# Moving the start of the weights' and the activations' buffers on the chip to multiples of 512 bytes, in a hybrid decoder layer

## The chip, the cores and the metric

The kernel runs on one core of a Trainium2 chip. The metric is the device time of one launch in microseconds, the median of several runs. Names of engines: PE is the matrix engine (PEld its weight load), DVE the vector engine, ACT the scalar engine, POOL the general engine, SP the engine that here only issues DMAs.

## The reference

One decoder layer on 256 tokens of width 2048, all in float32: a norm, one wide input projection, three branches (latent attention, gated linear attention, gated delta net), a gated merge of their projections, an output projection with residual, and a gated channel mixer with a causal convolution. Cut to the products, which are nearly all of the work:

```python
def token_mixer(h, ...):
    parts = jnp.split(h @ w_in, _split_points(), axis=-1)        # 2048 x 13408
    ...
    mixed = (g_mla * (y_mla @ w_branch_mla) + g_gla * (y_gla @ w_branch_gla)
             + g_gdn * (y_gdn @ w_branch_gdn))                   # three times 1024 x 2048
    return mixed @ w_out                                         # 2048 x 2048

def conv_ffn(h, w_up, conv_w, conv_b, w_down):
    gate, up = jnp.split(h @ w_up, 2, axis=-1)                   # 2048 x 11264
    gate = causal_dwconv(gate, conv_w) + conv_b
    return (jax.nn.silu(gate) * up) @ w_down                     # 5632 x 2048
```

## The kernel before, in words

Every large product is made of three: weights and activations are each split into a high and a low part of the type float32r (`hi`, `lo`), and high by high, high by low and low by high are added up in PSUM. A piece of weights is two k-tiles of 128 rows by 512 columns (`KP = 2`): SP loads it as `raw` (L183, helper `piece`), ACT casts `hi` (L190) and DVE takes `lo = raw - hi` (L103 through `tt`), and PE multiplies. `raw`, `hi` and `lo` have four buffers each in the pool `stream`. Three helpers issue the products:

- `t_chunk` (L246 to L248), tokens on the output's partitions: the stationary operand is a 128 x 128 block of the activations, the moving one 128 x 512 of the weights in `stream`. A chunk of 16 k-tiles is 96 matmuls. The whole program has 1,280 matmuls on each of the three lines.
- `fj_chunk` (L227, L228), for the up projection of the channel mixer: the stationary operand is a block of the weights in `stream`, the moving one the activations `hl_h`, 512 columns (high and low side by side) on L227 and 256 on L228, in turn. 1,408 pairs.
- `f_chunk` and others through `mm3` (L195 to L197), and the key and value products of the latent attention (L491 to L493): stationary blocks from `stream`, 256 moving columns from the activations, or the reverse; 492 matmuls on each of L195 to L197, 32 on each of L491 to L493.

A fourth loop stands at the end (L1165 to L1167): the last quarter-chunk of the down projection, 4 k-tiles, whose split weights `wl` were put into the buffers of the activations' pools beforehand, so that both of its operands come from there; 512 columns at a time for three quarters of the width, then twice 256, for each of the two token tiles.

On the chip a tile is a range of bytes in every one of 128 partitions. Pools lie one behind the other in the order in which they are opened: `const` (tiles made by `keep`), `stream`, `small` (tiles made by `small`), and then `slots`, `slots2` and the region pools, which hold all activations in slots of 2 KiB and, for some, 1 or 1.5 KiB. In the built program `stream` begins at byte 24,992 of the partition, which is 48 x 512 + 416, and `slots` at byte 85,024, which is 166 x 512 + 32. A slot of 2 KiB and a block of 128 columns of float32 (512 bytes) keep the offset within 512 bytes, so nearly every operand from `stream` begins at 416 and nearly every operand from the activations' pools at 32 modulo 512. In the last loop (L1165 to L1167) both operands begin at 32.

The order of instructions on each engine is set by the Tile framework's scheduler, which runs a simulated timeline when the program is built; it is not written by hand.

Of the kernel before, what the change touches and what calls it, by code (L numbers as in the profile page):

```python
# [16 lines left out]
P = 128  # L17
# [4 lines left out]
NSMALL = 5  # GLA levels within 32 positions  # L22
WARM = 8
FFN_PARTS = ((0, 4), (4, 8), (8, 10))  # of the 11 chunks of 512; the last one is left over
KP = 2  # k-tiles in a piece of weights

# column offsets of the combined input projection
# [5 lines left out]
def shape_constants():  # L33
    """Masks and tables that depend on the shapes alone: float columns and 0/1 masks."""
    i = np.arange(P)[:, None]
    j = np.arange(P)[None, :]
    ident = (i == j).astype(np.float32)
    tri = (i <= j).astype(np.float32)
    gt = (i > j).astype(np.float32)
    amask = np.where(j <= i, 0.0, -1e30).astype(np.float32)  # L40
    inv = 10000.0 ** (-np.arange(0, 64, 2, dtype=np.float64) / 64)
    cols = np.zeros((P, 2))
    cols[:, 0] = np.tile(inv, 4)
    cols[:, 1] = np.where((np.arange(P) % 64) < 32, -1.0, 1.0)
    # within a diagonal 32 x 32 block [j, i], twice: the identity and the levels' halves
    bj, bi = i % 32, np.tile(np.arange(32), 2)[None, :]
    masks = [bj == bi]
    for l in range(NSMALL):
        s = 1 << l
        masks.append((bi // (2 * s) == bj // (2 * s)) & ((bi // s) % 2 == 1) & ((bj // s) % 2 == 0))  # L50
    reset = np.broadcast_to(np.arange(T) % 64 != 0, (P, T))
    return (np.concatenate([ident, tri, gt, amask, cols], axis=1).astype(np.float32),
            np.concatenate(masks + [reset], axis=1).astype(np.float32))


def trunk(ctx, tc, A, out, dbg=None, stop=None):
# [14 lines left out]
    # Slots of 2 KiB a partition. A tag's slots are given out in program order, so that work which  # L71
    # runs side by side has tags of its own; the pools of the region follow each other on its bytes.
# [37 lines left out]
    def rsqrt(m, n):  # L110
        """[P, n] positive -> 1/sqrt, by the bit-level start and Newton steps."""
        y = small(n, "rsy", 4)
        dve.tensor_scalar(y.bitcast(I32), m.bitcast(I32), -0.5, 1597463007.0, op0=MUL, op1=ADD)
        mh = small(n, "rsm")
        dve.tensor_scalar(mh, m, -0.5, None, op0=MUL)
        for _ in range(3):
            a = small(n, "rsa")
            tt(a, y, y, MUL)
            tt(a, a, mh, MUL)
            y2 = small(n, "rsy", 4)  # L120
            stt(y2, a, 1.5, y, ADD, MUL)
            y = y2
        return y
# [4 lines left out]
    # ---------------------------------------------------------------- constants  # L128
# [3 lines left out]
    ident = keep([P, P], "ident")  # L132
# [22 lines left out]
    # the tensor engine's clock rises while the first loads are on their way  # L155
# [20 lines left out]
    # ---------------------------------------------------------------- weights  # L176
# [22 lines left out]
    def f_chunk(wv, c0, actv, n=512):  # L199
        """feature-major: list of PSUM banks, two [128, 256] tiles in each"""  # L200
        nf = n // P
        banks = [ACC() for _ in range((nf + 1) // 2)]
        nk = len(actv)
        for k0 in range(0, nk, KP):
            kk = min(KP, nk - k0)
            hi, lo = piece(wv[:, k0:k0 + kk, c0:c0 + n], kk, n)
            for f in range(nf):
                o = banks[f // 2][:, (f % 2) * 256:(f % 2) * 256 + 256]
                for kt in range(kk):
                    k = k0 + kt  # L210
                    ah, al = actv[k]
                    fs = slice(f * P, (f + 1) * P)
                    mm3(o, hi[:, kt, fs], lo[:, kt, fs], ah, al, k == 0 and f % 2 == 0, k == nk - 1)
        return banks

    def fj_chunk(wv, c0, joint, tag):
        """feature-major, by the joint parts [high | low] of 256 tokens each: a PSUM bank for each of four
        tiles, whose halves add up to the product"""
# [13 lines left out]
    def t_chunk(wv, c0, actv, n=512, ks=None):  # L232
        """token-major: one PSUM bank [128 tokens, n] for each token tile"""
# [20 lines left out]
    def pairs(n, tag, name):  # L254
        """n feature tiles [128, 256], two in each slot"""
        tiles = [S(tag, (P, 2, 256), n=name) for _ in range((n + 1) // 2)]
        return tiles, [tiles[i // 2][:, i % 2, :] for i in range(n)]

    class Act:
        """activations [n k-tiles of 128, 256 tokens] as the exact sum of two fp32r parts"""  # L260
# [11 lines left out]
        def add(self, full):  # L272
            """full: [128, 2, 256] fp32, the next two k-tiles"""
            hi, lo = self.new()
            act.copy(hi, full)
            tt(lo, full, hi, SUB)
# [4 lines left out]
    class Joint(Act):  # L281
        """the same with both parts of a k-tile in one slot"""
# [9 lines left out]
    def gained(psb, gains, store):  # L292
        """PSUM bank with two k-tiles [128, 256], times a per-partition gain each, split"""
# [8 lines left out]
    # ---------------------------------------------------------------- norm of x  # L302
    def row_stats(tiles, n):
        """tiles[t][c] [128, 512] -> sum of squares [128, 2]"""
# [14 lines left out]
    def row_bcast(r, o):  # L319
        """[128, 2] of the two token tiles -> [128, 256], the same on every partition"""  # L320
# [12 lines left out]
    # x times the gain of its norm; the rows' 1/rms comes in after the projections  # L333
# [36 lines left out]
    # ---------------------------------------------------------------- MLA projections  # L370
    # rotary tables on 4 groups of 32 partitions
# [52 lines left out]
    # rotary key, GLA's low-rank gate, GDN's beta and decay logits: one tile of 96 columns  # L424
# [11 lines left out]
    def rope(o, x, nq):  # L436
        """o[:32 nq] = rotary of x; x at the same partitions, in PSUM or at 0..63"""
# [16 lines left out]
    for hp in range(4):  # L454
        b0, b1 = ACC(), ACC()
        for k0 in range(0, 4, KP):
# [4 lines left out]
            # columns put in the order nope, nope, rope, rope  # L461
# [37 lines left out]
    # ---------------------------------------------------------------- MLA attention  # L499
# [49 lines left out]
    # ---------------------------------------------------------------- GDN projections  # L549
# [25 lines left out]
    # ---------------------------------------------------------------- GDN mixing  # L575
# [9 lines left out]
    def b3(ap, n):  # L585
        """[P, a] -> [P, a, n], repeated"""
# [18 lines left out]
    # sums of squares of q and k: row i for the i-th pair of tiles, then token-major  # L605
# [37 lines left out]
    # decay between positions j <= i from segment sums of the log decay: within the first and the second  # L643
    # half, and (second half's prefix) + (first half's suffix, as the exponential's bias)
# [40 lines left out]
    for g in range(4):  # L685
# [10 lines left out]
        # decayed q k of the blocks 00, 01 | 11 and decayed k k of the block 01, for both heads  # L696
# [10 lines left out]
    # inverses of the 32 x 32 unit-triangular diagonal blocks, transposed, by forward substitution:  # L707
    # partitions = (half of the columns, block, unit)
# [32 lines left out]
    # two groups of heads side by side, so that one's steps fill the other's waits  # L741
    for gp in ((0, 1), (2, 3)):
        # values token-major, over the norm of k
# [66 lines left out]
    # per-head norm: f = s rsqrt(s^2 ssq / 128 + eps)  # L810
# [13 lines left out]
    def gated_out(o_tiles, f_of, zs, gcol, name, ytag):  # L824
        """o token-major times its norm factor and gate -> feature-major, times gain, split"""
# [15 lines left out]
    def gates_of(c0, name, tag):  # L841
        """token-major 2 silu(z) / r of 1024 columns z of the input projection, r the rows' 1/rms"""
# [10 lines left out]
    # ---------------------------------------------------------------- merge  # L853
# [3 lines left out]
    def merge(b, y, w, c, first=False, last=False):  # L857
        """512 columns of a branch's projection, times its gate, into the sum"""
# [39 lines left out]
    # ---------------------------------------------------------------- GLA projections  # L898
# [15 lines left out]
    # ---------------------------------------------------------------- GLA mixing  # L914
# [6 lines left out]
    # log gates feature-major, and their running sums from each start of 64 positions  # L921
# [23 lines left out]
    def halves(ap, s):  # L945
        """[P, 256] -> the left and the right halves [P, blocks, s] of blocks of 2 s"""
# [5 lines left out]
    for hd in range(4):  # L952
        q, k, cb = lqv[hd], lkv[hd], sums[hd]
        # exponents: from each block's middle, and of the two chunks from the boundary between them
# [24 lines left out]
        # products [j, i]: diagonal 32 x 32 blocks of the small levels and of q k itself, then levels 5 and 6  # L979
# [64 lines left out]
    # ---------------------------------------------------------------- output projection, residual  # L1044
# [39 lines left out]
    # ---------------------------------------------------------------- channel mixer  # L1084
# [56 lines left out]
    # the last part goes by token tiles, so that the first one's norm and stores run under the second's  # L1141
    # products; its weights stay on chip
# [14 lines left out]
    for t in range(2):  # L1157
# [22 lines left out]
        # three Newton steps for -8 / sqrt(m): y <- (y y m / 4^i - 3) y is -2 times the usual one  # L1180
# [60 lines left out]
```

## Time and profile before

| | |
|---|---|
| time, median of 3 runs | 1707.05 us (1706.93 to 1707.15) |
| span of the profiled execution | 1705.8 us, granted PE clock 0.997 of full speed |
| around the span | 1.25 us between it and the median of the runs |
| busy share of the span: PE, PEld | 99%, 84% |
| DVE, ACT, POOL | 64%, 48%, 5% |
| DMA | 308.71 MB, 181 GB/s mean |

A profiled execution has no device time of its own beside its span, so the sums below are made against the span of 1705.8 us and then put on the median of the runs. "Busy" for PE counts from a matmul's start to its modelled end, and the ends overlap the next starts: the duration of one matmul is no measure of what it costs. What it costs is the distance from its start to the next start, and that is read from the timeline.

### The profile page before, as it was taken

What the parts mean: (1) busy time and instruction counts of PE and PEld (TensorE: products, weight loads), DVE (VectorE), ACT (ScalarE), POOL (GpSimd) and SP (SyncE); (2) the same over time, 40 slices, a digit from 0 to 9 for tenths busy, and PEclk for the clock granted to TensorE, in tenths of its full rate; (3) what the DMA queues carried; (4) which work ended last, traced back from release to release, by engine and by line L of the source; (5) the groups of instructions that cost most, each with busy time, mean ns of one, the idle gap of its engine ahead of it and who ended that gap; (6) DMA issues with size and microseconds to landing.
All of it is one profiled execution on the core that took longest, in us unless ns stands there. A gap on an engine that the chain in (4) does not pass through costs nothing.

```text
span 1705.8 us, 24609 instructions
## 1 busy us (share of the span) xinstructions
PE 1692.2 (99%) x9516; PEld 1438.3 (84%) x9516; DVE 1095.1 (64%) x1709; ACT 819.0 (48%) x1132; POOL 88.9 (5%) x132
## 2 busy tenths in 40 slices
PE   9999999999999999999999999999999999999997
PEld 7999988878988788888888888888888888888886
DVE  6856887855744695655555666664466665466666
ACT  6554553333444564444444455553355553345454
POOL 1000013200000000000000000000000000000000
PEclk9999999999999999999999999999999999999999
DMA  7554456654455465556655666655565556655653
GB/s 259 156 187 136 149 161 185 200 156 146 153 185 185 150 196 172 173 179 205 197 196 186 201 187 189 191 186 186 187 193 188 185 186 188 193 186 186 189 186 119
DMA packets 166277, 308.71 MB, mean 181 GB/s; under 512 B 16826, under 2 KB 19570, under 8 KB 166160
## 3 DMA queue, kind: packets, MB, share of 16 engines
q1 hardware_dynamic: 163200, 301.83, 56.4%
q0 software_dynamic: 2928, 5.30, 1.1%
q8 instruction: 74, 1.21, 0.3%
q14 instruction: 43, 0.35, 0.1%
q10 hardware_dynamic: 32, 0.01, 0.0%
HBM read 304.48 MB, written 2.62 MB: 180 GB/s over the span
## 4 chain that ended last, share of the span: by engine, by line
PE 99%; DMA 0%; ACT 0%; DVE 0%; SPq 0%; ACTq 0%; issue 0%
PE acc L247 18%; PE acc L248 18%; PE acc L246 18%; PE acc L227 10%; PE mix L227 10%; PE acc L228 5%; PE mix L228 5%; PE acc L197 3%; PE acc L195 3%; PE acc L196 3%; PE ps L511 0%; PE acc L1165 0%; PE acc L1167 0%; PE acc L1166 0%; PE ps L510 0%; DMA x<-in_x_dram 0%
## 5 line engine op out<-in xcount | busy, mean ns | idle before, releaser
L103 DVE TENSOR_TENSOR lo<-raw,hi 128x1024 fp32r<-128x1024 f32 (+2 forms) x571 | 687.1, 1205 | 540.7 <-ACT hi L190 537.5
L190 ACT CAST hi<-raw 128x1024 fp32r<-128x1024 f32 (+2 forms) x555 | 581.1, 1047 | 753.8 <-PE acc L248 437.1
L247 PE MATMUL acc<-lo,hi_h 128*128 128x512 f32 x640 | 254.0, 398 | 0.0
L248 PE MATMUL acc<-hi,lo_h 128*128 128x512 f32 x640 | 252.7, 397 | 0.0
L246 PE MATMUL acc<-hi,hi_h 128*128 128x512 f32 x640 | 251.4, 397 | 0.7 <-ACT hi L190 0.7
L227 PE MATMUL mix<-hl_h,hi 128*128 128x512 f32 x704 | 247.7, 393 | 0.0
L227 PE MATMUL acc<-hl_h,hi 128*128 128x512 f32 x704 | 247.5, 394 | 0.0
L228 PE MATMUL mix<-hl_h,lo 128*128 128x256 f32 x704 | 199.1, 283 | 0.0
L228 PE MATMUL acc<-hl_h,lo 128*128 128x256 f32 x704 | 198.6, 283 | 0.0
L227 PEld LDWEIGHTS mix<-hl_h,hi 128*128 128x128 f32 x704 | 132.2, 188 | 30.5
L227 PEld LDWEIGHTS acc<-hl_h,hi 128*128 128x128 f32 x704 | 131.9, 188 | 30.1
L246 PEld LDWEIGHTS acc<-hi,hi_h 128*128 128x128 f32 x640 | 120.7, 189 | 29.0 <-ACT hi L190 1.3
L247 PEld LDWEIGHTS acc<-lo,hi_h 128*128 128x128 f32 x640 | 120.9, 189 | 27.7 <-DVE lo L103 0.4
L248 PEld LDWEIGHTS acc<-hi,lo_h 128*128 128x128 f32 x640 | 120.6, 189 | 27.3
L228 PEld LDWEIGHTS acc<-hl_h,lo 128*128 128x128 f32 x704 | 132.3, 188 | 0.6
L228 PEld LDWEIGHTS mix<-hl_h,lo 128*128 128x128 f32 x704 | 132.4, 188 | 0.0
L247 PE MATMUL acc<-lo,hi_f 128*128 128x512 f32 x320 | 126.1, 394 | 0.0
L246 PE MATMUL acc<-hi,hi_f 128*128 128x512 f32 x320 | 125.9, 395 | 0.0
L248 PE MATMUL acc<-hi,lo_f 128*128 128x512 f32 x320 | 125.7, 394 | 0.0
L197 PE MATMUL acc<-hi_h,lo 128*128 128x256 f32 (+1 forms) x400 | 113.6, 284 | 0.0
L195 PE MATMUL acc<-hi_h,hi 128*128 128x256 f32 (+1 forms) x400 | 113.6, 284 | 0.0
L196 PE MATMUL acc<-lo_h,hi 128*128 128x256 f32 (+1 forms) x400 | 113.4, 284 | 0.0
(390 smaller groups left out, 2238.8 us busy)
## 6 DMA issues: line engine op xcount, KB each, us to landing
raw<-in_w_in_dram SPq DMA_DIRECT2D x207, 512.0 KB, 3.5
raw<-in_ffn_w_up_dram SPq DMA_DIRECT2D x176, 512.0 KB, 4.1
raw<-in_ffn_w_down_dram SPq DMA_DIRECT2D x88, 512.0 KB, 4.6
raw<-in_w_out_dram SPq DMA_DIRECT2D x32, 512.0 KB, 3.8
raw<-in_w_branch_mla_dram SPq DMA_DIRECT2D x16, 512.0 KB, 3.7
raw<-in_w_branch_gdn_dram SPq DMA_DIRECT2D x16, 512.0 KB, 3.7
raw<-in_w_branch_gla_dram SPq DMA_DIRECT2D x16, 512.0 KB, 3.8
raw<-in_mla_w_ukv_dram SPq DMA_DIRECT2D x8, 512.0 KB, 4.4
```

Of the source, the lines that this page charges most:

```text
L103: (eng or dve).tensor_tensor(o, a, b, op=op)
L190: act.copy(hi[:, ks], raw[:, ks])
L195: pe.matmul(o, s_hi, m_hi, start=first, stop=False, skip_group_check=True)
L196: pe.matmul(o, s_hi, m_lo, start=False, stop=False, skip_group_check=True)
L197: pe.matmul(o, s_lo, m_hi, start=False, stop=last, skip_group_check=True)
L227: pe.matmul(banks[f], hi[:, kt, fs], joint[k], start=k == 0, stop=False, skip_group_check=True)
L228: pe.matmul(banks[f][:, :T], lo[:, kt, fs], joint[k][:, :T], start=False, stop=k == nk - 1, skip_group_check=True)
L246: pe.matmul(o, ah, hi[:, kt, :], start=first, stop=False)
L247: pe.matmul(o, ah, lo[:, kt, :], start=False, stop=False)
L248: pe.matmul(o, al, hi[:, kt, :], start=False, stop=last)
```

## The change

One tile of the pool `const` is made 24 columns (96 bytes) wider, of which the first 128 columns are used as before, and one tile of 95 columns is added to the pool `small` and set to zero by POOL, so that it is used at all. Apart from these two lines the change takes away comments and docstrings.

```diff
-    ident = keep([P, P], "ident")
+    ident = keep([P, P + 24], "ident")[:, :P]
+    pool.memset(small(95, "room", 1), 0.0)
     sync.dma_start(ident, cst[:, 0:P])
```

In the built program `stream` now begins at byte 25,088 = 49 x 512 and `slots` at byte 85,504 = 167 x 512, and all slots of the activations at the same distances behind it as before; what begins at 416 and what begins at 32 modulo 512 now begins at 0. Tiles of `const` move by 96 bytes (except `ident` itself). One line is added, so lines from 133 on have numbers greater by one.

The scheduler gives the same instructions on SP in the same order. On PE, DVE and ACT the order differs only in the first part of the program, up to the rotary tables and the query latent; from there on all rows are the same. Three places of that follow.

ACT, the first casts and normalised activations, before (`hi_318` is the high part of the first weights, `hi_h_140` and `hi_h_151` the first activations, `junk` the sum of squares of x):

```order
L650 CAST maskr<-ones 128x128
L649 CAST maskr<-rest 128x128
L309 ACTIVATE junk_224,st_223<-x_106 128x512
L299 ACTIVATE hi_h_140<-ps_135,ac 128x256
L190 CAST hi_318<-raw_110 128x512
L299 ACTIVATE hi_h_151<-ps_146,ac 128x256
L190 CAST hi_318<-raw_110 128x512
L299 ACTIVATE hi_h_140<-ps_135,ac 128x256
```

and now:

```order
L651 CAST maskr<-ones 128x128
L310 ACTIVATE junk_226,st_225<-x_108 128x512
L191 CAST hi_320<-raw_112 128x512
L300 ACTIVATE hi_h_142<-ps_137,ac 128x256
L191 CAST hi_320<-raw_112 128x512
L300 ACTIVATE hi_h_153<-ps_148,ac 128x256
L300 ACTIVATE hi_h_142<-ps_137,ac 128x256
```

The first weight cast now stands ahead of the first activation instead of behind it, and the copy of `rest` has left this place (it comes later on ACT).

POOL, the first DMAs, before (`rest` holds masks and the rotary columns, `prow` the gains):

```order
L1237 UNCONDITIONAL_BRANCH
L145 DMA rest<-in_cst_dram 128x386
L141 DMA prow_82<-in_ffn_norm_dram 16x128
L141 DMA prow_82<-in_mla_q_norm_dram 4x128
L141 DMA prow_82<-in_mla_kv_norm_dram 4x128
```

and now:

```order
L1238 UNCONDITIONAL_BRANCH
L133 MEMSET room_79 128x95
L142 DMA prow_84<-in_ffn_norm_dram 16x128
L142 DMA prow_84<-in_mla_q_norm_dram 4x128
L142 DMA prow_84<-in_mla_kv_norm_dram 4x128
L142 DMA prow_84<-in_gla_out_norm_dram 8x128
L142 DMA prow_84<-in_gdn_out_norm_dram 8x128
L142 DMA prow_84<-in_gdn_conv_w_dram 64x128
L146 DMA rest<-in_cst_dram 128x386
```

The memset is new at the head of the queue, and the load of `rest` has gone behind the six loads of `prow`.

## Rows read from the trace of the kernel before

**Rows 1.** The page's parts 1 and 4: busy time, chain that ended last

```profile
PE 1692.2 (99%) x9516; PEld 1438.3 (84%) x9516; DVE 1095.1 (64%) x1709; ACT 819.0 (48%) x1132; POOL 88.9 (5%) x132
...
PE 99%; DMA 0%; ACT 0%; DVE 0%; SPq 0%; ACTq 0%; issue 0%
```

**Rows 2.** Waits of PE: us in total, times, longest

```profile
PE acc L1165 <- ACT hi_f L275: 1.1, 1, 1.1
PE warm L158 <- DVE ones L154: 1.1, 1, 1.1
PE ps L340 <- DMA x<-in_x_dram: 0.7, 1, 0.7
PE acc L246 <- ACT hi L190: 0.7, 1, 0.7
```

**Rows 3.** Timeline of PE: start us, us; `t_chunk`'s stretch of 384 matmuls, first and last

```profile
483.42 0.39 PE L246 MATMUL acc<-hi,hi_h 128*128 128x512 f32 x1
...
572.41 0.39 PE L248 MATMUL acc<-hi,lo_h 128*128 128x512 f32 x1
```

**Rows 4.** The same for `fj_chunk`: first of 512 pairs, next line's first start

```profile
1223.79 0.40 PE L227 MATMUL acc<-hl_h,hi 128*128 128x512 f32 x1
...
1403.52 0.40 PE L246 MATMUL acc<-hi,hi_f 128*128 128x512 f32 x1
```

**Rows 5.** Windows: us; PE, PEld, DVE, ACT, POOL busy (x); PEclk, DMA share, GB/s

```profile
460.00:483.00 23.00, 23.00 (x196) 23.00 (x195) 12.65 (x16) 9.99 (x13) 0.00 (x0) 1.00 0.58 186
484.00:572.00 88.00, 88.00 (x381) 71.32 (x380) 43.26 (x39) 37.41 (x39) 0.00 (x0) 1.00 0.61 189
1230.00:1400.00 170.00, 170.00 (x970) 149.00 (x969) 112.61 (x142) 89.28 (x120) 11.33 (x8) 1.00 0.60 188
1688.00:1692.00 4.00, 4.00 (x19) 3.30 (x18) 3.49 (x16) 2.01 (x8) 0.00 (x0) 1.00 0.00 0
```

**Rows 6.** Timeline of PE in the last loop, second token tile

```profile
1687.44 0.40 PE L1165 MATMUL acc<-wl,hi_f 128*128 128x512 f32 x1
1687.68 0.40 PE L1166 MATMUL acc<-wl,hi_f 128*128 128x512 f32 x1
1687.91 0.39 PE L1167 MATMUL acc<-wl,lo_f 128*128 128x512 f32 x1
...
1688.61 0.39 PE L1167 MATMUL acc<-wl,lo_f 128*128 128x512 f32 x1
1688.83 0.39 PE L1165 MATMUL acc<-wl,hi_f 128*128 128x512 f32 x1
...
1692.91 0.28 PE L1165 MATMUL acc<-wl,hi_f 128*128 128x256 f32 x1
...
1693.14 0.28 PE L1167 MATMUL acc<-wl,lo_f 128*128 128x256 f32 x1
...
1695.66 0.28 PE L1167 MATMUL acc<-wl,lo_f 128*128 128x256 f32 x1
```

**Rows 7.** Timeline of PE: shortest distances in `fj_chunk` and in the last loop

```profile
1002.20 0.39 PE L227 MATMUL acc<-hl_h,hi 128*128 128x512 f32 x1
1002.42 0.28 PE L228 MATMUL acc<-hl_h,lo 128*128 128x256 f32 x1
...
1685.53 0.28 PE L1166 MATMUL acc<-wl,hi_f 128*128 128x256 f32 x1
1685.64 0.28 PE L1167 MATMUL acc<-wl,lo_f 128*128 128x256 f32 x1
```

**Rows 8.** Timelines of ACT and POOL: the start, and a memset of POOL

```profile
6.94 0.47 ACT L299 ACTIVATE hi_h<-ps,ac 128x256 fp32r<-128x256 f32 x1 [0.42 <-PE ps L340]
7.31 0.61 ACT L190 CAST hi<-raw 128x512 fp32r<-128x512 f32 x1
...
7.30 0.17 POOL L607 MEMSET sel<- 128x68 f32 x1
```

## The prediction

> **What bounds the kernel.** I read the page first: PE is busy for 99% of the span and the chain that ended last is PE for 99% [rows 1]. Then the waits of PE: four of them, 3.6 us in all, at the very start and at the last loop [rows 2]. So no transfer, cast or subtraction decides the time; only what one matmul costs does. [...]
>
> - `t_chunk`, 512 columns: 384 matmuls, 383 distances in 572.41 - 483.42 = 88.99 us [rows 3], 0.2324 us each (0.23235 unrounded).
> - `fj_chunk`, 512 and 256 columns in turn: 512 pairs in 1403.52 - 1223.79 = 179.73 us [rows 4], 0.3510 us a pair.
> - 256 columns from L195 to L197: 196 matmuls touch the window from 460 to 483 us [rows 5], two of which began before it; 194 in 23.00 us is 0.1186 us.
> - The last loop, once it has settled: 18 matmuls of 512 columns in 1692.91 - 1688.83 = 4.08 us, 0.2267 us each, and 21 of 256 columns in 1695.66 - 1693.14 = 2.52 us, 0.1200 us each [rows 6].
>
> The last loop is what I build on. It does the same three products as `t_chunk`, with operands of the same shapes and types, and takes 5.7 ns less for each. DVE is busy for 3.49 of 4.00 us beside it, more densely than beside `t_chunk` [rows 5], so idle neighbours are not the reason. Two things differ: its weights lie in the activations' pools, so that the moving and the stationary operand both begin at 32 modulo 512, where `t_chunk` streams from 416 against blocks at 32; and no DMA runs beside it (share 0.00 against 0.61) [rows 5]. The difference between the two widths, 226.7 - 120.0 = 106.7 ns for 256 columns, is 0.417 ns a column, one per period of 2.4 GHz; so every matmul pays something on top of its columns: 13.3 ns in the last loop, 232.35 - 213.3 = 19 ns in `t_chunk`, (351.0 - 320.0) / 2 = 15.5 ns in `fj_chunk`, 118.6 - 106.7 = 12 ns on L195 to L197. The change can move only this part, and it is paid some 8,200 times.
>
> **The change part by part.** My theory is that the part on top depends on where the two operands begin relative to each other within 512 bytes, because the next weight load reads while the columns stream. After the change all of them begin at 0, so their relation is that of the last loop, and I give them its numbers.
>
> - `t_chunk`: 3 x 1,280 = 3,840 matmuls, 232.35 to 226.67 ns, gives 3,840 x 5.68 = 21.8 us less. Settling costs something: after a change of width the last loop took 1688.83 - 1687.44 = 1.39 us for six [rows 6] against 1.36. At most 40 chunks have to settle, 40 x 0.03 = 1.2 us; I take 1.5.
> - `fj_chunk`: 1,408 pairs, 351.04 to 226.67 + 120.00 = 346.67 ns, gives 6.2 us less. The widths alternate here, so it may never settle; the bounds are 0 and 6.2 and I take 6.2, since in the last loop the long first distance after a change of width (0.24) and the short one the other way (0.11) [rows 6, 7] nearly cancel.
> - L195 to L197 and L491 to L493: 3 x 492 + 3 x 32 = 1,572 matmuls, 118.6 to 120.0 ns, 2.2 us more; bounds 0 and 2.2.
> - The weights' DMAs now land at multiples of 512 bytes. Whatever that gives them is hidden: PE waited for a DMA once, 0.7 us, for x at the start [rows 2]. I cost it at nothing; it could give back those 0.7 us at most.
> - The memset on POOL: the nearest row is one of 128 x 68 at 0.17 us [rows 8]; the six loads of `prow` start that much later, and `rest` behind them about 3 us later. Their users come tens of microseconds later on PE. Nothing, unless ACT should stand at the copy of `rest`.
> - The order at the start: ACT's first cast of weights now stands ahead of the first activation. ACT idled for 0.42 us before that activation and the cast takes 0.61 us [rows 8]. If the weights have landed by then, the first product comes up to 0.6 us earlier; if not, ACT holds the activation back, by perhaps 1 us. I take 0, with bounds of -0.6 and +1.0.
>
> Sum: -21.8 + 1.5 - 6.2 + 2.2 = -24.3 us, so a span of 1681.5 us, and on the median of the runs 1707.05 - 24.3 = 1682.7 us. The bounds of the terms make it 1678 (the 256 columns unchanged, nothing paid for settling, 0.6 and 0.7 us gained at the start) to 1691 (`fj_chunk` unchanged, settling twice as dear, 1 us lost at the start).
>
> **The rivals.**
>
> *No change (about 1707).* The last loop's gain comes from the absent DMA, or from the place of its buffers in the large, or the distances are an affair of PE alone. For it: DMA share and operand offsets change together between the stretches [rows 5], so the trace cannot part them, and engine and DMA are otherwise independent here (PE does not wait). Against it: when the DMA is equally absent, right after a change of width, the distances are 0.24, 0.23 us and settle only later [rows 6], so a quiet DMA does not bring 0.2267 by itself. [...]
>
> *Much faster (about 1616).* Not the relation alone counts but a start at a round address: both before and after, relation or not, every operand of the old kernel begins at 32 modulo 128, so the trace has no row of an aligned one. The best it could show is the shortest distances seen: 0.22 us for 512 columns and 0.11 us for 256 [rows 7]. Then `t_chunk` gives 3,840 x 12.35 = 47.4 us, the pairs 1,408 x 21 = 29.6, the rest 1,572 x 8.6 = 13.5; 90.5 in all. For it: these distances occur, so what is paid on top is not fixed. Against it: the last loop, once settled, does not use them. [...]
>
> *Slower (about 1725).* With both operands beginning at 0, the weight load and the columns meet head-on at every start, and the kernel stays where the last loop is just after a change of width: 1687.91 - 1687.44 = 0.47 us for two, 0.235 each [rows 6]. Then 3,840 x 2.65 = 10.2, pairs of 0.235 + 0.120 us 1,408 x 4 = 5.6, and 2.2 on the rest: 18 us more. The point from which it decides is a mean of 232.35 ns for 512 columns. Against it: the last loop has both operands at the same offset, and settles.
>
> **How the numbers follow.** What a measurement of this kernel can tell from no change is about 0.2%, 3.4 us. Forecast 0.52; no change 0.22; much faster 0.10; slower 0.12; the remaining 0.04 for only one of the terms coming true, between 1691 and 1703. Faster by over 0.2%: 0.52 + 0.10 + 0.04 = 0.66; within: 0.22; slower: 0.12. The range from 1670 to 1710 takes in the forecast with its bounds, the part between, and no change; the forecast's own range is 1678 to 1691.
>
> **What would show it.** In the timeline of the changed kernel, the stretch of 384 matmuls of `t_chunk` should take 87.0 us where it took 89.0, the 512 pairs of `fj_chunk` 177.5 where they took 179.7, and the last loop should be as it was, 0.2267 and 0.1200 us. If the distances are unchanged and the time too, the relation of the offsets was not the cause; if the last loop itself becomes shorter, the absolute start counts; if 512 columns take more than 232.35 ns, the starts collide. PE's waits should stay under 5 us in all; if they grow, I have misjudged the start.

## The result and the profile after

The changed kernel takes 1685.96 us (median of 4 runs, 1684.95 to 1686.28), the kernel before beside it 1707.10 us (1706.93 to 1707.19): a ratio of 0.9873, 95% interval [0.9861, 0.9884], so 21.1 us less. The profiled execution has a span of 1682.8 us where it was 1705.8, 23.0 us less. The forecast was 1682.7 us with a range from 1670 to 1710, 1678 to 1691 for the likeliest case, and a span of 1681.5 us.

PE still sets the end. From the page of the changed kernel, busy time (part 1) and the chain that ended last (part 4), which answer to [rows 1]:

```profile
PE 1669.3 (99%) x9516; PEld 1431.9 (85%) x9516; DVE 1094.0 (65%) x1709; ACT 820.6 (49%) x1132; POOL 89.5 (5%) x133
...
PE 99%; DMA 0%; ACT 0%; DVE 0%; SPq 0%; ACTq 0%; issue 0%
```

Its waits of PE (us in total, times, longest), to be held against [rows 2]:

```profile
PE acc L247 <- ACT hi_h L300: 1.4, 2, 0.9
PE acc L1166 <- ACT hi_f L276: 1.1, 1, 1.1
PE warm L159 <- DVE ones L155: 1.1, 1, 1.1
```

They are 3.6 us as before: the same 9,516 matmuls simply start closer together. PE's timeline of the changed kernel (start us, us) has the stretches of [rows 3] and [rows 4], lines one higher, and ahead of them 202 products of 256 columns:

```profile
454.76 0.36 PE L198 MATMUL acc<-hi_h,lo 128*128 128x256 f32 x1
...
478.95 0.28 PE L198 MATMUL acc<-hi_h,lo 128*128 128x256 f32 x1
479.07 0.40 PE L247 MATMUL acc<-hi,hi_h 128*128 128x512 f32 x1
...
565.91 0.39 PE L249 MATMUL acc<-hi,lo_h 128*128 128x512 f32 x1
...
1207.69 0.39 PE L228 MATMUL acc<-hl_h,hi 128*128 128x512 f32 x1
...
1385.25 0.39 PE L247 MATMUL acc<-hi,hi_f 128*128 128x512 f32 x1
```

The 384 matmuls of `t_chunk` take 565.91 - 479.07 = 86.84 us from first to last start where they took 88.99: 0.2267 us each instead of 0.2324. The 512 pairs of `fj_chunk` take 1385.25 - 1207.69 = 177.56 us where they took 179.73. Both are the numbers that the prediction asked for (87.0 and 177.5). The 202 products of 256 columns are 201 distances in 24.19 us, 120.3 ns each. A window of the changed kernel (us; busy (x) of PE, PEld, DVE, ACT, POOL; PEclk, DMA share, GB/s) answers to [rows 5]:

```profile
484.00:560.00 76.00, 76.00 (x337) 62.92 (x336) 38.27 (x35) 33.33 (x34) 0.00 (x0) 1.00 0.67 192
```

The DMA share beside `t_chunk` is 0.67 now, no less than the 0.61 before, and the distances are 0.2267 us all the same; the granted clock is 1.00, as it was.

The last loop is as it was. PE's timeline, where answers to [rows 6] stand:

```profile
1665.84 0.39 PE L1166 MATMUL acc<-wl,hi_f 128*128 128x512 f32 x1
...
1669.92 0.28 PE L1166 MATMUL acc<-wl,hi_f 128*128 128x256 f32 x1
...
1670.15 0.28 PE L1168 MATMUL acc<-wl,lo_f 128*128 128x256 f32 x1
...
1672.67 0.28 PE L1168 MATMUL acc<-wl,lo_f 128*128 128x256 f32 x1
```

18 matmuls of 512 columns in 1669.92 - 1665.84 = 4.08 us and 21 of 256 in 1672.67 - 1670.15 = 2.52 us, as before to the last digit.

Summed over all distances between PE's starts in the two timelines, kind by kind (us):

| kind of matmul | count | before | after | difference | forecast |
|---|---|---|---|---|---|
| `t_chunk`, 512 columns | 3,840 | 900.59 | 879.35 | -21.24 | -20.3 |
| `fj_chunk`, 512 and 256 in turn | 1,408 pairs | 495.95 | 493.23 | -2.72 | -6.2 |
| 256 columns (L195 to L197, L491 to L493 of before) | 1,572 | 190.13 | 191.76 | +1.63 | +2.2 |
| last loop | 120 | 22.26 | 22.26 | 0 | 0 |
| all others | 1,168 | 85.67 | 85.02 | -0.65 | 0 |
| sum | | | | -22.98 | -24.3 |

One row is off: the pairs. They run at two paces in the changed kernel. From its timeline, the first matmul of the second and of the eighth `fj_chunk` in the first part of the mixer, and the same two in the second part (384 pairs between the two each time):

```profile
962.30 0.40 PE L228 MATMUL mix<-hl_h,hi 128*128 128x512 f32 x1
...
1097.98 0.40 PE L228 MATMUL mix<-hl_h,hi 128*128 128x512 f32 x1
...
1229.94 0.39 PE L228 MATMUL mix<-hl_h,hi 128*128 128x512 f32 x1
...
1363.06 0.39 PE L228 MATMUL mix<-hl_h,hi 128*128 128x512 f32 x1
```

135.68 / 384 = 353.3 ns a pair in the first part, 133.12 / 384 = 346.7 ns in the second. Before it was 351.1 ns in both. So 512 pairs became 2 ns dearer and only the other 896 got what was forecast.

### The profile page after: what moved, and what is told of

It reads as the page before. It is cut to its first block, busy times and chain, and to the rows that moved or that the text cites. A ratio compares the mean times of both kernels' runs of the same rounds, so it can differ in the third digit from the quotient of the medians.

```text
span 1682.8 us, 24609 instructions
## 1 busy us (share of the span) xinstructions
PE 1669.3 (99%) x9516; PEld 1431.9 (85%) x9516; DVE 1094.0 (65%) x1709; ACT 820.6 (49%) x1132; POOL 89.5 (5%) x133
## 4 chain that ended last, share of the span: by engine, by line
PE 99%; DMA 0%; ACT 0%; DVE 0%; SPq 0%; ACTq 0%; issue 0%
PE acc L249 17%; PE acc L247 17%; PE acc L248 17%; PE acc L228 10%; PE mix L228 10%; PE acc L229 5%; PE mix L229 5%; PE acc L198 3%; PE acc L196 3%; PE acc L197 3%; PE ps L512 0%; PE acc L1166 0%; PE acc L1168 0%; PE acc L1167 0%; PE ps L511 0%; DMA raw<-in_w_in_dram 0%
## 5 line engine op out<-in xcount | busy, mean ns | idle before, releaser
L248 PE MATMUL acc<-lo,hi_h 128*128 128x512 f32 x640 | 249.5, 392 | 0.0
L249 PE MATMUL acc<-hi,lo_h 128*128 128x512 f32 x640 | 248.9, 391 | 0.0
L247 PE MATMUL acc<-hi,hi_h 128*128 128x512 f32 x640 | 247.5, 392 | 1.4 <-ACT hi_h L300 1.4
L247 PEld LDWEIGHTS acc<-hi,hi_h 128*128 128x128 f32 x640 | 120.0, 188 | 27.1 <-ACT hi_h L300 2.1
L248 PEld LDWEIGHTS acc<-lo,hi_h 128*128 128x128 f32 x640 | 120.2, 188 | 24.6 <-DVE lo L103 0.2
L247 PE MATMUL acc<-hi,hi_f 128*128 128x512 f32 x320 | 124.2, 389 | 0.0
L197 PE MATMUL acc<-lo_h,hi 128*128 128x256 f32 (+1 forms) x400 | 113.9, 285 | 0.0
```

Of the source, the lines that this page charges most:

```text
L197: pe.matmul(o, s_hi, m_lo, start=False, stop=False, skip_group_check=True)
L247: pe.matmul(o, ah, hi[:, kt, :], start=first, stop=False)
L248: pe.matmul(o, ah, lo[:, kt, :], start=False, stop=False)
L249: pe.matmul(o, al, hi[:, kt, :], start=False, stop=last)
```

## The experiments

In all of them "relation" means the start of the activations' slots less the start of the weights' `hi` and `lo`, modulo 256 bytes. In the kernel before it is 128 (slots at 32, weights at 416, modulo 512), in the changed kernel 0. The pool `small` lies between the two, so the size of its unused tile sets the relation alone. All kernels compute the whole layer.

### Is it the relation, or the round start?

*Both at 32, nothing aligned* (on the kernel before: the slots stay where they are relative to 512 bytes, the weights' `hi` and `lo` move behind a gap, the tiles that the DMAs fill stay at 416):

```diff
+    pool.memset(small(96, "room", 1), 0.0)
...
+    pool.memset(wp.tile([P, 32], F32, name="gap", tag="gap", bufs=1), 0.0)
```

> The weights as loaded (raw) stay at 416 modulo 512, as before the change; their split parts hi and lo and all activations' slots begin at 32 modulo 512. Nothing but the relation of the two operands is changed: it is 0, and no pool begins at a multiple of 512. Relation theory: the stretch of 384 matmuls of t_chunk takes 87.0 us (226.7 ns each), 256 columns 120.0 ns, the time is that of the changed kernel, 1685 us within 2. Theory that a start at a round address counts: 89.0 us for the stretch as before (232.4 ns), time about 1707. Theory that the landing place of the DMA counts: the same, 1707.

*Both aligned to 128, but 128 apart* (on the changed kernel):

```diff
-    pool.memset(small(95, "room", 1), 0.0)
+    pool.memset(small(127, "room", 1), 0.0)
```

> The changed kernel with the activations' slots 128 bytes further: weights at 0, activations at 128 modulo 512. That is the relation of the kernel before (32 - 416 = 128 modulo 512), with both operands at multiples of 128. Relation theory: t_chunk at 232.4 ns (89.0 us for 384), pairs of fj_chunk at 351 ns, 256 columns at 118.6 ns, time 1705 to 1708. Theory that round starts (64 or 128 bytes) count, or the DMA's landing place: 226.7 ns and 1685 us.

The first takes 1685.51 us (ratio to before 0.9871 [0.9856, 0.9885]), the second 1706.56 us (0.9993 [0.9983, 1.0002]). PE's timeline of the first, the 384 matmuls of `t_chunk`, first and last:

```profile
479.21 0.40 PE L248 MATMUL acc<-hi,hi_h 128*128 128x512 f32 x1
...
566.05 0.39 PE L250 MATMUL acc<-hi,lo_h 128*128 128x512 f32 x1
```

and of the second:

```profile
483.95 0.39 PE L247 MATMUL acc<-hi,hi_h 128*128 128x512 f32 x1
...
572.94 0.39 PE L249 MATMUL acc<-hi,lo_h 128*128 128x512 f32 x1
```

86.84 us without any round start, 88.99 us with round starts but the old relation. The whole gain comes with the relation and none of it with the alignment. Since the DMAs' targets stay at 416 in the first, where the weights land plays no part either. The second has the changed kernel's order of instructions on PE, the same in all 9,516 places, so the new order at the start does not make the gain. The reads and writes of the other engines do not explain the longer distances either: of the 1,149 distances in the three stretches of 384 matmuls of the kernel before, 79 lie where no instruction of ACT, DVE or POOL runs, and they average 232.6 ns against 232.3 for the rest.

### What period, and what do the other relations cost?

Seven more sizes of the same tile (`small(103)` for 32 bytes, then 111, 119, 135, 143, 151, and 159 for 256), one execution each.

> The changed kernel with the activations' slots 32 bytes further: weights at 0, activations at 32 modulo 512. A look at how fine the relation counts. If only the relation modulo some larger unit counts (128 bytes or more between different places), 32 bytes change nothing: 226.7 ns and 1685 us. If every byte of the relation counts, t_chunk comes out between 213 and 241 ns, the shortest and longest that a distance could be by the rows of before; the time goes by 3.84 us for each ns.

> The changed kernel with the activations' slots 256 bytes further: the relation is 256 modulo 512. If the two reads disturb each other where they meet in the same part of 512 bytes, half of it away should be the best or the worst relation: t_chunk under 226.7 ns (then the time falls under 1685) or over 232.4 (over 1707). If only relation 0 settles and all others run loose, 230 to 234 ns and about 1705.

> The changed kernel with the activations' slots 64 bytes further. Relation theory, as it stands after relation 0 and 256 alike (226.7 ns in t_chunk), 128 (232.4) and 32 (233.3): a value of its own, the same in every stretch. If the last loop (both operands from the activations' pools) changes too, the theory is wrong. Prediction by neighbours: t_chunk between 232 and 234 ns, time 1700 to 1708.

> The changed kernel with the activations' slots 96 bytes further. By neighbours 64 and 128: t_chunk 232 to 234 ns, time 1700 to 1708; the last loop as ever, 226.7 and 120.0 ns.

> The changed kernel with the slots 160 bytes past the weights modulo 256, the last place in steps of 32. Theory (it lies between 128 with 232.4 ns and 192 with 228.9 for 512 columns, and 119.1 and 113.8 for 256): 229 to 233 ns and 114 to 119 ns, 1690 to 1707 us. If the order of the places means nothing, any value from 1685 to 1716.

> The changed kernel with the activations' slots 192 bytes further, by a period of 256 the same as 64 bytes less. If only the size of the relation counts, as with 64; if its sign counts (which of the two operands is ahead), t_chunk, which streams the weights, and fj_chunk, which streams the activations, change places against the run with 64.

> The changed kernel with the activations' slots 224 bytes further, by a period of 256 the same as 32 bytes less. With 32 bytes more t_chunk took 233.3 ns, the pairs of fj_chunk 346.7 and 256 columns 117.1. If the sign counts, t_chunk (streaming the weights) should now be at a relation of +32 as the activations' streams were, and be quicker than 226.7 by the 3 ns that 256 columns gained against 120.0: about 223.7 ns, 1674 us. If the size alone counts, 1702 us again.

All distances in ns, from first and last starts in PE's timelines: 384 matmuls of `t_chunk` in one stretch, a stretch of 202 of 256 columns, and 384 pairs in the first part of the mixer and in the second. The times are single executions except at 0 and 128.

| relation | `t_chunk` | 256 columns | pairs, first / second part | time, us |
|---|---|---|---|---|
| 0 (changed) | 226.7 | 120.3 | 353.3 / 346.7 | 1685.96 |
| 256 | 226.7 | 120.3 | 353.3 / 346.7 | 1685.68 |
| 32 | 233.3 | 117.1 | 346.7 / 346.7 | 1702.28 |
| 64 | 233.3 | 118.2 | 353.3 / 348.9 | 1708.39 |
| 96 | 234.3 | 120.4 | 350.0 / 350.0 | 1715.51 |
| 128 (before) | 232.4 | 119.1 | 351.1 / 351.1 | 1707.10 |
| 160 | 233.3 | 119.1 | 346.7 / 346.7 | 1703.42 |
| 192 | 228.9 | 113.8 | 353.3 / 353.3 | 1691.74 |
| 224 | 233.3 | 118.7 | 353.3 / 353.3 | 1710.39 |

The dearest relation, 96, in PE's timeline, first and last of the 384:

```profile
487.19 0.39 PE L247 MATMUL acc<-hi,hi_h 128*128 128x512 f32 x1
...
576.91 0.40 PE L249 MATMUL acc<-hi,lo_h 128*128 128x512 f32 x1
```

and the one best for 256 columns, 192, a stretch of 202 of them:

```profile
450.78 0.37 PE L198 MATMUL acc<-hi_h,lo 128*128 128x256 f32 x1
...
473.66 0.28 PE L198 MATMUL acc<-hi_h,lo 128*128 128x256 f32 x1
```

At 256 bytes every number of relation 0 is back: the period is 256 bytes, not the 512 in which the prediction reckoned. The last loop, whose two operands keep their relation in all of these kernels, takes 22.2 to 22.3 us over its 120 distances in every one of them. The distances of the table account for the time where each kind keeps one pace. At 96 they give, against before, 3,840 x 1.9 + 1,572 x 1.3 - 1,408 x 1.1 = 7.3 + 2.0 - 1.5 = 7.8 us more; measured against the kernel before, run beside it, are 1715.51 - 1707.81 = 7.7 us. At 192 and 224 they give 18.4 us less and 6.2 us more, where 16.1 less and 2.6 more were measured, since other stretches run at other paces: 301 products of 256 columns at 116.9 ns at 192, the pairs of the third part of the mixer at 346.8 at 224.

No simple law of the relation shows: its mirror images (32 and 224, 64 and 192) differ. Five of these seven expectations missed. At 256 none of the outcomes named came, neither the best nor the worst relation nor a loose one. At 64 `t_chunk` came as the neighbours had it and the time 0.4 us above their range; at 96 the time was 7.5 us above it. At 192 neither the size alone counts (it is not as 64) nor do `t_chunk` and the pairs change places. At 224 the miss is 8 us at the least (1710.39 us against 1674 or 1702). At 160, 256 columns came at 119.1 ns and the time at 1703.42 us, inside what the neighbours gave, and `t_chunk` at 233.3, just past their edge.

### Two paces at one relation

What decides between 353.3 and 346.7 ns a pair? In the first `fj_chunk` of the mixer PE also issues small products of other lines, which the scheduler puts between the pairs. PE's timeline of the changed kernel around them:

```profile
944.15 0.39 PE L228 MATMUL acc<-hl_h,hi 128*128 128x512 f32 x1
...
947.61 0.39 PE L228 MATMUL acc<-hl_h,hi 128*128 128x512 f32 x1
947.84 0.61 PE L326 MATMUL ps<-dg,ones 128*128 128x128 f32 x4
...
955.48 0.24 PE L1091 MATMUL ps<-ident,frow 88*128 88x88 f32 x1
955.51 0.48 PE L228 MATMUL acc<-hl_h,hi 128*128 128x512 f32 x1
```

From 944.15 to 947.61 there are ten pairs: 346 ns each, the quick pace, in the same chunk and with operands at the same places modulo 256. After the last small product, at 955.48, the pairs run at 353.3 for the rest of the part. So the pace is not a property of the place or of the part.

The second part changes its pace too. Its start in the changed kernel, right behind a settled stretch of `t_chunk`:

```profile
1207.69 0.39 PE L228 MATMUL acc<-hl_h,hi 128*128 128x512 f32 x1
...
1210.51 0.64 PE L228 MATMUL acc<-hl_h,hi 128*128 128x512 f32 x2
...
1211.33 0.40 PE L229 MATMUL acc<-hl_h,lo 128*128 128x256 f32 x2
1211.57 0.40 PE L228 MATMUL acc<-hl_h,hi 128*128 128x512 f32 x1
...
1213.99 0.39 PE L228 MATMUL acc<-hl_h,hi 128*128 128x512 f32 x1
```

The first eight pairs take 1210.51 - 1207.69 = 2.82 us, 352.5 ns each, the slow pace. Then the order of the widths breaks (two of 512 columns in a row, a little later two of 256), and the next seven take 1213.99 - 1211.57 = 2.42 us, 345.7 ns each, and the pace stays quick to the end of the part.

*The widths apart once* (on the changed kernel; `settle` is true at c == 0, which comes once, in the very first `fj_chunk`, not in every part as the expectation has it):

```diff
-            for f in range(4):
+            for part in ((2, 1) if settle and k0 == 2 else (3,)):
+                for f in range(4):
...
-                    pe.matmul(banks[f], hi[:, kt, fs], joint[k], start=k == 0, stop=False, skip_group_check=True)
+                        if part & 1:
+                            pe.matmul(banks[f], hi[:, kt, fs], joint[k], start=k == 0, stop=False, skip_group_check=True)
```

(the product of 256 columns stands under `if part & 2` in the same way).

> The changed kernel; only in the first fj_chunk of each FFN part the eight products of 256 columns at the second piece are issued together, and then the eight of 512, so that the alternation of widths starts anew from a settled stretch of 512 columns. No work more or less. In the changed kernel the pairs of the first FFN part (512 pairs) take 353.3 ns and those of the later parts 346.7. Theory (the alternation has two steady patterns, and what stands ahead of it chooses one): the first part goes to 346.7 ns, 512 x 6.67 = 3.4 us less, about 1682.5 us. Rival (the place in the program or the work beside it sets the pattern): the pairs stay at 353.3 ns, 1686 us.

1685.28 us, ratio 0.9874 [0.9857, 0.9890]: no gain over the changed kernel. Its timeline, the second and the eighth `fj_chunk`:

```profile
962.71 0.40 PE L230 MATMUL mix<-hl_h,hi 128*128 128x512 f32 x1
...
1098.39 0.40 PE L230 MATMUL mix<-hl_h,hi 128*128 128x512 f32 x1
```

135.68 us, the slow pace. On PE the widths stand apart in two groups. The first is soon followed by small products (from 942.59 us). The second is followed by undisturbed pairs, and these answer the question:

```profile
944.75 0.75 PE L232 MATMUL acc<-hl_h,lo 128*128 128x256 f32 x5
945.34 1.31 PE L230 MATMUL acc<-hl_h,hi 128*128 128x512 f32 x5
...
946.60 0.40 PE L230 MATMUL acc<-hl_h,hi 128*128 128x512 f32 x1
...
948.01 0.40 PE L230 MATMUL acc<-hl_h,hi 128*128 128x512 f32 x1
...
949.16 0.39 PE L230 MATMUL acc<-hl_h,hi 128*128 128x512 f32 x1
...
953.67 0.39 PE L230 MATMUL acc<-hl_h,hi 128*128 128x512 f32 x1
```

Right behind the settled products of 512 columns, four pairs take 948.01 - 946.60 = 1.41 us, 352.5 ns each: the slow pace, not the quick one that was expected. Behind four small products (at 948.25 us), thirteen pairs take 953.67 - 949.16 = 4.51 us, 347 ns each, and behind the next small products, at 954.25 and 955.89, the pairs are slow again and stay so.

### A place for each kind

*Two places* (on the kernel before): `hi` and `lo` stand in one tile, whose contents begin at relation 0 for `t_chunk` and `fj_chunk`, and 64 bytes later, at relation 192, for `f_chunk` and the query and 96-column products. To make room, `sel` moves into the region's tag `Pm`.

```diff
+OFF = 16
...
+    pool.memset(small(32, "room", 1), 0.0)
...
+    def high_low(kk, n, off):
+        hl = wp.tile([P, 2112], F32R, name=nm("hl"), tag="hl")
+        return (hl[:, o:o + kk * n].rearrange("p (k c) -> p k c", k=kk) for o in (off, 1024 + off))
...
-            hi, lo = piece(wv[:, k0:k0 + kk, c0:c0 + n], kk, n)
+            hi, lo = piece(wv[:, k0:k0 + kk, c0:c0 + n], kk, n, OFF)
```

> From the kernel before: hi and lo stand in one tile, and its contents begin at the slots' place modulo 256 bytes (relation 0) for t_chunk and fj_chunk and 64 bytes further (weights to slots: 192) for the products of 256 columns in f_chunk and the 96-column part. Theory (the relation alone sets what is paid on top, for each kind of matmul by itself): t_chunk stays at 226.7 ns, the 256 columns go from 120.3 to the 113.8 ns of the run with relation 192, about 1,476 x 6.5 = 9.6 us less than the changed kernel, about 1676 us, with fj_chunk as in the changed kernel. Rival (a relation acts through the whole allocation, or the joint tile holds its buffer longer): the 256 columns stay at 119 to 120 ns, 1686 us, or PE's waits grow beyond 5 us.

1677.56 us, ratio 0.9825 [0.9810, 0.9839]: 8.4 us below the changed kernel, whose interval [0.9861, 0.9884] lies above this one. Its timeline, 201 products of 256 columns, the 384 of `t_chunk` behind them, and the second and eighth `fj_chunk`:

```profile
452.34 0.37 PE L200 MATMUL acc<-hi_h,hl 128*128 128x256 f32 x1
...
475.11 0.28 PE L202 MATMUL acc<-hi_h,hl 128*128 128x256 f32 x1
475.22 0.40 PE L251 MATMUL acc<-hl,hi_h 128*128 128x512 f32 x1
...
562.06 0.39 PE L253 MATMUL acc<-hl,lo_h 128*128 128x512 f32 x1
...
958.35 0.39 PE L232 MATMUL mix<-hl_h,hl 128*128 128x512 f32 x1
...
1091.47 0.39 PE L232 MATMUL mix<-hl_h,hl 128*128 128x512 f32 x1
```

113.8 ns for 256 columns and 226.7 for `t_chunk` in one kernel: each kind follows the relation of its own operands. Over all 1,572 products the gain is 191.76 - 186.11 = 5.65 us instead of the 9.6 expected, for two reasons that the distances show. 207 of them lie between 119.5 and 122.5 ns, most of them those of the key and value expansion, which stayed at relation 0; half of these the 9.6 had counted in by mistake. And at relation 192 there are two paces as well: 887 products at 113 to 115 ns, 428 (some 20 of them not from such a place) at 116 to 119, by whole stretches. The last two rows bring the other part of the gain, unexpected: the pairs of the first part run at 133.12 / 384 = 346.7 ns, at the same relation 0 at which they ran at 353.3 in the changed kernel, 493.23 - 490.11 = 3.12 us less over all pairs. Together 8.8 us; `t_chunk` and the rest give 1.8 us back, and the span is 1682.8 - 1675.8 = 7.0 us shorter. That the time came near the 1676 us expected is partly luck: the products of 256 columns gave less than was reckoned, and the pairs, from which nothing was expected, made up for most of it.

*Both edits together:*

> The two before together: relation 0 for t_chunk and fj_chunk, 192 for the products of 256 columns, and the first fj_chunk of each FFN part with its widths apart at the second piece. If both theories hold the savings add: 9.6 + 3.4 us below the changed kernel, about 1673 us; if only one holds, 1676 or 1682.5.

1676.93 us, ratio 0.9822 [0.9807, 0.9837], the same as the two places alone: the pairs were at 346.7 already, so there was nothing left for the second edit. Here too four pairs behind the settled products of 512 columns are slow, 944.43 - 943.02 = 1.41 us, before small products follow.

What sets the pace thus stands as follows. It is shown that one relation has more than one steady pace, and that the same pairs change it in the middle of a chunk, behind a few small products or behind a break in the order of the widths. The theory of *the widths apart once*, that a settled stretch of 512 columns ahead brings the quick pace, is refuted: behind such a stretch the pairs were slow at first, in both runs with that edit and at the start of every part of the mixer in the changed kernel. Behind a break either pace can follow, and what decides between them stays open.

## Why the prediction was right, and where it was off

- **The bound** (PE alone, nothing else late): right. Waits 3.6 us before and after, PE 99%.
- **The theory** (the part on top of the columns depends on the relation of the two starts): right, shown by the two kernels that part relation from alignment. Two things in it do not stand so: the period is 256 bytes, not 512, and the reason given (the next weight load reads while the columns stream) is still only argued: in the kernel before a load of 0.19 us for L247 does start at 483.42 us, together with the matmul of L246 ahead of it, but no run isolates a weight load. The "2.4 GHz" beside the 0.417 ns a column is only its reciprocal; the traces give the clock as a share of full speed.
- **`t_chunk`** (-21.8, +1.5 for settling): the distance came out as forecast, 0.2267 us, in the middle of the program and beside running DMAs. The sum is -21.24, 0.9 us more than forecast, but about 1.4 us of it are a lower clock in the profiled execution of the kernel before (below). Without them it is -19.9, 0.4 short of the forecast.
- **`fj_chunk`** (-6.2, bounds 0 and 6.2): this is the term that was mis-sized; it measured -2.7. The step that failed is "since in the last loop the long first distance after a change of width and the short one the other way nearly cancel": adding the two settled distances held for 896 pairs, 346.7 ns as written, and failed for the 512 of the first part, at 353.3. 512 x 6.67 = 3.4 us, which is the miss of 3.5 us. The prediction did say that alternating widths may never settle, but took the upper bound. It was luck that the 512 pairs which it named as a sign lie in the second part: in the first part the same sign would have failed.
- **256 columns** (+2.2): 120.0 ns as forecast once settled (in the stretch above the 200 distances behind the first take 23.99 us). With the long first distance, the four longest stretches went from 118.9 to 119.4 ns before to 120.2 to 120.7, 1.3 ns each, as forecast; the shorter stretches, half of the products, moved less, and the sum is +1.63.
- **The start** (0, bounds -0.6 and +1.0): a gain, and a little outside. ACT's timeline of the changed kernel, where [rows 8] has the old order:

```profile
6.23 0.62 ACT L191 CAST hi<-raw 128x512 fp32r<-128x512 f32 x1 [0.83 <-DMA raw<-in_w_in_dram]
6.75 0.47 ACT L300 ACTIVATE hi_h<-ps,ac 128x256 fp32r<-128x256 f32 x1
```

  The cast that moved ahead does hold ACT, 0.83 us for its DMA, as feared; but the copy of `rest` no longer stands before x, and the first activation begins at 6.75 where it began at 6.94 us. PE's first product comes at 7.27 instead of 7.97 us. The granted clock differs too. A window of the kernel before and the same one of the changed kernel (columns as above):

```profile
9.00:12.00 3.00, 3.00 (x8) 2.33 (x8) 2.81 (x5) 2.16 (x5) 0.45 (x1) 0.50 1.02 285
```

```profile
9.00:12.00 3.00, 2.58 (x13) 1.91 (x14) 2.63 (x5) 2.40 (x6) 0.19 (x1) 1.00 1.05 403
```

  The kernel before has here a granted clock of 0.50; PE had stood idle for 0.75 and 0.74 us ahead of its products at 6.35 and 7.97 us. The changed kernel, idle for 0.92 and 0.50 us ahead of those at 7.27 and 9.42, keeps 1.00. What lowers the clock no run shows. From 9.21 to 12.20 us seven matmuls of 512 columns take 2.99 us where seven at 0.2324 us take 1.63: 1.4 us. With the 0.7 us of the first product this makes 2.1 of the 2.4 us (58.69 - 56.29) by which the first 256-column product starts earlier. The lower clock is not bound to the old order: the profiled execution at relation 96, which has the new one, shows it as well (0.50 from 8 to 11 us). The kernel with the old relation and the new order (1706.56 us, an interval that takes in no change) shows no gain in time from the start.
- **DMA and memset** (nothing): PE's wait for a DMA, 0.7 us in [rows 2], is gone, and nothing is late behind the memset.
- **The median**: the sum was made on the span and missed it by 1682.8 - 1681.5 = 1.3 us. That it was so little is luck: without the 1.4 us of the lower clock the distances give 21.6 us less instead of 23.0, near the 21.1 us of the medians, and the sum, 24.3 us, misses by 2.7. The other 2 us of the 3.3 by which the median missed lie between span and median: 1.25 us before, 1685.96 - 1682.8 = 3.2 us now, since the execution with this span was the quickest of the four (1684.95 us).

The rivals. *No change* falls with the DMA share of 0.67 beside 0.2267 us, and with the time moving from 1685 to 1715 us while nothing but the size of an unused tile changes. *Much faster* by round starts falls with the kernel at 32 bytes, which is as fast as the aligned one; the shortest steady distance of 512 columns alone that the runs show was 226.7 ns. *Slower by head-on starts* falls with the last loop's distances holding at relation 0; a relation that is slower does exist (96, 234.3 ns), but it is not 0.

## What to carry to other kernels

Where one engine is busy all the time, read the distances between its starts in each long stretch and compare stretches that do the same work: a difference of 2.4% between two of them (232.4 and 226.7 ns) was a gain that no busy share shows. For these float32 products as two parts, try the place of the streamed operand relative to the stationary one in steps of 32 bytes within 256, for each kind of product by itself; an alignment to 512 as such was worth nothing, and the relation was worth 1.3%, or 1.8% with a place for each kind. Where widths alternate, forecast a range: settled distances of the single widths did not add up in every stretch.

## What was not expected of the hardware

- The distance from start to start of the same matmul depends on the operands' relation modulo 256 bytes, from 226.7 to 234.3 ns for 512 columns and from 113.8 to 120.4 ns for 256, and each width has its best relation at another place (0 and 192).
- The relation has a sign: 64 gives 233.3 and 118.2 ns, 192 gives 228.9 and 113.8.
- At one relation there are several steady paces, which hold over hundreds of matmuls and through whole parts of the program: 353.3 or 346.7 ns a pair at 0, 113 or 118 ns for 256 columns at 192. A few other products between them, or two of one width in a row, can change the pace.
- The settled distances lie on a grid: 113.3, 120.0, 226.7, 233.3, 346.7 and 353.3 ns are 17, 18, 34, 35, 52 and 53 times 6.67 ns, which is 16 times the 0.417 ns a column by which the two widths differ in the last loop. The 232.4 ns of `t_chunk` before and its 228.9 at relation 192 are means of a repeating series: 228, 230, 233, 241, 232, 231 and 232 ns, and 226, 229 and 232 ns. No run shows why.
